# Issuing the last store of a ReLU row-sum kernel from ScalarE instead of SyncE

## The chip, the cores and the metric

The kernel runs on one core of a Trainium2 chip. A core has several engines with instruction streams of their own: VectorE (DVE in the profile), ScalarE (ACT), GpSimd (POOL), TensorE (PE, not used here) and SyncE (SP), which computes nothing and issues DMA transfers. Sixteen DMA engines move the data between HBM and the core's on-chip memory. The streams are ordered against each other by semaphores alone: an instruction can wait until a semaphore has reached a count, and can add to one when it is done; a DMA adds 16 in all when its data has landed.

The metric is the device time of one execution in microseconds, the median over several runs.

## The reference

```python
def setup_inputs():
    batch, seq, dim = 32, 512, 1024
    return {
        "x": np.random.randn(batch, seq, dim).astype(np.float32),
    }

def reference(x: np.ndarray) -> np.ndarray:
    relu_x = np.maximum(x, 0)
    return np.sum(relu_x, axis=-1).astype(np.float32)
```

Every one of the 32 x 512 = 16384 rows of 1024 floats is clamped at zero and summed. 64 MiB are read and 64 KiB are written.

## The kernel before

The rows lie over 128 partitions, 128 rows a partition: sixteen of them from the first eighth of the input, the other 112 from the rest. They are loaded in blocks of 16 rows a partition (8 MiB a load) into three buffers in turn (line 185, `load`); block 3 and those after it wait until VectorE has finished with the buffer. For most blocks ScalarE clamps in place (line 144) and VectorE sums with a reduction (line 152). Towards the end the loads become smaller, 8 and 4 rows (lines 208 to 218), and single rows are clamped and summed in one instruction, by ScalarE (line 159) or VectorE (line 167) alternately.

The last four rows of a partition are cut by hand so that little work is left once the last bytes have landed. Their first two rows and a piece of the third come in one load (line 228); two further pieces are loaded and summed in part by both engines (lines 237 to 243, `act_part` and `dve_part`, lines 121 and 126); the last piece, 403 elements, goes into the buffer `last` (line 244), beside the partial sums. GpSimd clamps one piece ahead (line 234). When all of that is there (`all_there`, line 253), VectorE finishes the sum of row NT - 2 with one instruction (line 254) and ScalarE that of row NT - 1 (line 263). Both add 1 to the semaphore `sems.end`, which then stands at 16 + 5 + 2.

All DMAs are issued by SyncE, in the order of its stream: thirteen loads and then three stores of the sums, from the tile `res` to the output (`store`, lines 110 to 118). The first store holds the first 16 sums of a partition, the second the next 110 and the third the last two (line 264). The third waits for `sems.end` at 16 + 5 + 2. All three add to `sems.stored`.

Behind the last store SyncE goes on to the end block, which is written by hand and holds two instructions: the clear of all the semaphores but `stored` (line 50), which must not happen before the last wait on `sems.end` is over, and a wait until all stores have landed, which also sets `stored` back to zero (line 51):

```python
    nc.sync.sem_clear(cleared)
    nc.sync.wait_ge(sems.stored, 16 * n_stores).then_inc(sems.stored, -16 * n_stores)
```

There are no barriers between the engines in the program; the first load is moved ahead of the program's opening (line 52).

Of the kernel before, what the change touches and what calls it, by code (L numbers as in the profile page):

```python
# [30 lines left out]
def kernel(tc: tile.TileContext, x: bass.AP, out: bass.AP):  # L31
    nc = tc.nc
    sems = Semaphores(tc)

    tc.close()
    tc.compile()
    nc.cur_bb = nc.bb_map[tc.start_bb_name]
    body = nc.cur_bb.bb.instructions
    ends = list(body)
    body.clear()  # L40
    n_stores = relu_sum(nc, sems, x, out)
    body.extend(ends)


    nc.cur_bb = nc.bb_map[tc.start_bb_name + "_end"]
    nc.cur_bb.bb.instructions.clear()
    nums = sorted(s.num for s in (*sems.loads, sems.act, sems.dve))
    cleared = range(nums[0], nums[-1] + 1)
    assert len(cleared) == len(nums)
    nc.sync.sem_clear(cleared)  # L50
    nc.sync.wait_ge(sems.stored, 16 * n_stores).then_inc(sems.stored, -16 * n_stores)
    open_without_barrier(tc, EARLY)


class Semaphores:
    def __init__(self, tc: tile.TileContext):
        n = len(TWO) + len(TAIL) + 4
        self.loads = [tc.alloc_semaphore(f"load{i}") for i in range(n)]
        self.act = tc.alloc_semaphore("act")
        self.dve = tc.alloc_semaphore("dve")  # L60
        self.end = self.loads[-1]
        self.stored = tc.alloc_semaphore("stored")


def relu_sum(nc, sems: Semaphores, x: bass.AP, out: bass.AP):
    x_flat = x.flatten_outer_dims()
    N, D = x_flat.shape
    NT = N // P
# [20 lines left out]
    def rows(m, n):  # L89
        if m < ROWS:  # L90
            return xf[:, m : m + n, :]
        return xv[:, m - ROWS : m - ROWS + n, :]

    def sums(m, n):
        if m < ROWS:
            return of[:, m : m + n], res[:, m : m + n]
        return ov[:, m - ROWS : m - ROWS + n], res[:, m : m + n]
# [12 lines left out]
    def store(m, n, act, sem, count):  # L110
        nonlocal n_store
        dst, src = sums(m, n)
        if act:
            nc.sync.wait_ge(sems.act, act)
        nc.sync.dma_start(out=dst, in_=src).wait_op(sem, count, "sem-ge").then_inc(
            sems.stored, 16
        )
        n_store += 1

    def act_part(ap, accum_out, after):  # L120
        nc.scalar.activation(out=ap, in_=ap, func=RELU, accum_out=accum_out).wait_op(  # L121
            *after, "sem-ge"
        ).then_inc(sems.end, 1)
# [84 lines left out]
    for n in TAIL:  # L208
# [12 lines left out]
    src = rows(m, 4).rearrange("p c d -> p (c d)")  # L221
# [13 lines left out]
        out=clamped, in0=clamped, scalar1=0.0, scalar2=None, op0=MAX  # L235
    ).wait_op(loaded, 16, "sem-ge").then_inc(sems.end, 1)
    for lo, hi, n, first, second in (
# [17 lines left out]
        out=clamped,  # L255
# [5 lines left out]
        accum_out=res[:, NT - 2 : NT - 1],  # L261
    ).wait_op(*all_there, "sem-ge").then_inc(sems.end, 1)
    act_part(last[:, 2 + LAST_DVE :], res[:, NT - 1 : NT], all_there)
    store(NT - 2, 2, 0, sems.end, 16 + 5 + 2)
    return n_store


def open_without_barrier(tc: tile.TileContext, n_loads: int):
# [46 lines left out]
```

## Time and profile before

| What | Value |
|---|---|
| Time, median of 3 runs | 160.91 us (160.89 to 160.95) |
| Span of the profiled execution, first to last instruction | 159.7 us |
| Median less that span | 1.2 us |
| VectorE busy | 118.8 us (74%) |
| ScalarE busy | 103.6 us (65%) |
| GpSimd busy | 1.0 us (1%) |
| DMA | 67.18 MB, one queue, 98.0% of 16 engines' span |
| Last store, 1.0 KB: issue to landing | 1.4 us |

The profiled execution's own time is known as its span, from its first to its last instruction; what lies around the span, start-up and close-down, is in the time of the runs and not in the span. Rows that begin with SPq are instructions of SyncE's sequencer: DMA issues, waits and semaphore operations. The length of a DMA issue is the time that the sequencer needs to hand it over and not that of the transfer, for which the profile gives the time from the issue to the landing.

### The profile page before, as it was taken

How to read it: one execution, taken by the hardware profiler on the slowest of the kernel's cores; microseconds unless marked ns; L12 is line 12 of the kernel's file. 1: busy time of each engine (PE TensorE's matmuls, PEld its weight loads, DVE VectorE, ACT ScalarE, POOL GpSimd, SP SyncE). 2: the span in 40 equal slices, each digit the busy share in tenths (PEclk: the TensorE clock that was granted, in tenths of full speed). 3: DMA queues.
4: the chain of work that ended last, by engine and by line, in shares of the span. 5: the costliest groups of instructions: out<-in, count | busy, mean ns of one | idle time of the engine just before them, and what ended most of it. 6: DMA issues, size and time to landing. Idle time of an engine off the chain costs nothing.

```text
span 159.7 us, 125 instructions
## 1 busy us (share of the span) xinstructions
DVE 118.8 (74%) x44; ACT 103.6 (65%) x53; POOL 1.0 (1%) x5
## 2 busy tenths in 40 slices
DVE  0000000006999799999999999999999799999986
ACT  0000049993699808996099951999329993496995
POOL 0000000000000000000000000000000000000001
DMA  7996996996997997979969969969969969898993
GB/s 263 525 525 263 525 509 279 525 509 279 525 476 312 525 443 345 525 328 460 525 279 509 525 263 525 525 263 525 509 279 525 492 295 525 353 435 386 407 409 128
DMA packets 2304, 67.18 MB, mean 421 GB/s; under 512 B 640, under 2 KB 768, under 8 KB 1024
## 3 DMA queue, kind: packets, MB, share of 16 engines
q1 hardware_dynamic: 2304, 67.18, 98.0%
HBM read 67.11 MB, written 0.07 MB: 421 GB/s over the span
## 4 chain that ended last, share of the span: by engine, by line
DVE 45%; DMA 45%; ACT 9%; SPq 1%; issue 0%
DMA io<-in_x_dram 45%; DVE res L152 43%; ACT io L144 9%; DVE io L167 1%; SPq L103 1%; DVE io L126 1%; DVE io L254 0%
## 5 line engine op out<-in xcount | busy, mean ns | idle before, releaser
L152 DVE TENSOR_REDUCE res<-io 128x8 f32<-128x8192 f32 (+2 forms) x10 | 101.1, 10175 | 38.9 <-ACT io L144 38.9
L144 ACT ACTIVATE io<-io 128x8192 f32<-128x8192 f32 (+2 forms) x10 | 81.8, 8218 | 25.9 <-DMA io<-in_x_dram 25.9
L159 ACT ACTIVATE io<-io 128x1024 f32<-128x1024 f32 x18 | 18.8, 1043 | 6.6 <-DMA io<-in_x_dram 6.6
L167 DVE TENSOR_SCALAR_CACHE_REDUCE io<-io 128x1024 f32<-128x1024 f32 x14 | 16.2, 1214 | 0.5 <-DMA io<-in_x_dram 0.4
L142 ACT ACT_TABLE_LOAD x1 | 1.3, 1283 | 22.0 <-DMA io<-in_x_dram 22.0
L159 ACT ACTIVATION_READ_ACCUMULATOR io<-io 128x1 f32 x18 | 3.4, 187 | 0.0
L234 POOL TENSOR_SCALAR io<-io 128x254 f32<-128x254 f32 x1 | 0.8, 840 | 155.1 <-DMA io<-in_x_dram 155.1
L167 DVE DVE_READ_ACCUMULATOR io<-io 128x1 f32 x14 | 1.1, 82 | 0.0
L126 DVE TENSOR_SCALAR_CACHE_REDUCE io<-io 128x552 f32<-128x552 f32 (+1 forms) x2 | 1.1, 596 | 0.0
L121 ACT ACTIVATE io<-io 128x321 f32<-128x321 f32 (+1 forms) x2 | 0.9, 426 | 0.1
L254 DVE SCALAR_TENSOR_TENSOR io<-last,io 128x254 f32<-128x254 f32 x1 | 0.4, 425 | 0.0
L121 ACT ACTIVATION_READ_ACCUMULATOR io<-io 128x1 f32 x2 | 0.4, 187 | 0.0
L121 ACT ACTIVATE last<-last 128x153 f32<-128x153 f32 x1 | 0.3, 332 | 0.0
L121 ACT ACTIVATION_READ_ACCUMULATOR last<-last 128x1 f32 x1 | 0.2, 187 | 0.0
L126 DVE DVE_READ_ACCUMULATOR io<-io 128x1 f32 x2 | 0.2, 84 | 0.0
L299 POOL MEMSET const-bfloat16-1.0<- 128x1 bf16 x1 | 0.1, 101 | 0.0
L299 POOL MEMSET const-uint8-127<- 128x1 uint8 x1 | 0.1, 101 | 0.0
L299 POOL MEMSET const-float32-0.0<- 128x1 f32 x1 | 0.1, 99 | 0.2 <-issue 0.2
L299 POOL MEMSET const-float32-1.0<- 128x1 f32 x1 | 0.1, 98 | 0.0
L254 DVE DVE_READ_ACCUMULATOR io<-last,io 128x1 f32 x1 | 0.1, 83 | 0.0
## 6 DMA issues: line engine op xcount, KB each, us to landing
io<-in_x_dram SPq DMA_DIRECT2D x1, 4096.0 KB, 23.8
io<-in_x_dram SPq DMA_DIRECT2D x1, 2048.0 KB, 28.3
io<-in_x_dram SPq DMA_DIRECT2D x1, 1151.0 KB, 30.6
io<-in_x_dram SPq DMA_DIRECT2D x1, 436.5 KB, 31.2
io<-in_x_dram SPq DMA_DIRECT2D x1, 259.0 KB, 31.4
last<-in_x_dram SPq DMA_DIRECT2D x1, 201.5 KB, 31.4
io<-in_x_dram SPq DMA_DIRECT2D x7, 29.1
out_dram<-res SPq DMA_DIRECT2D x1, 55.0 KB, 1.6
```

The costliest lines, as they stand in the source:

```text
L103: dma = nc.sync.dma_start(out=dst, in_=src)
L121: nc.scalar.activation(out=ap, in_=ap, func=RELU, accum_out=accum_out).wait_op(*after, "sem-ge").then_inc(sems.end, 1)
L126: i = nc.vector.tensor_scalar(out=ap, in0=ap, scalar1=0.0, scalar2=None, op0=MAX, op1=ADD, accum_out=accum_out,)
L142: nc.scalar.preload_act_table(RELU).wait_op(loaded, 16, "sem-ge")
L144: i = nc.scalar.activation(out=ap, in_=ap, func=RELU)
L152: nc.vector.tensor_reduce(out=res[:, m : m + n], in_=ap, axis=mybir.AxisListType.X, op=ADD).wait_op(sems.act, n_act, "sem-ge").then_inc(se ...
L159: i = nc.scalar.activation(out=ap, in_=ap, func=RELU, accum_out=accum_out)
L167: i = nc.vector.tensor_scalar(out=ap, in0=ap, scalar1=0.0, scalar2=None, op0=MAX, op1=ADD, accum_out=accum_out,)
L234: nc.gpsimd.tensor_scalar(out=clamped, in0=clamped, scalar1=0.0, scalar2=None, op0=MAX).wait_op(loaded, 16, "sem-ge").then_inc(sems.end, 1)
L254: nc.vector.scalar_tensor_tensor(out=clamped, in0=last[:, : 2 + LAST_DVE], scalar=0.0, in1=clamped, op0=MAX, op1=ADD, accum_out=res[:, NT ...
L299: nc = _bacc.Bacc("TRN2", target_bir_lowering=False, num_devices=1)
```

## The change

The third store is no longer issued by SyncE but by ScalarE, from ScalarE's own DMA queue, with the same wait on `sems.end` and the same count on `sems.stored`. SyncE no longer knows by its own wait that `sems.end` is done with; so a new semaphore, `issued`, is added. ScalarE adds 1 to it behind the issue, and SyncE waits for that 1 and takes it back, before it goes on to the clear and to the final wait. The new semaphore is not among those that line 50 clears. SyncE's stream has two stores instead of three, and the count of stores that the final wait asks for is still three.

```diff
@@ -60,6 +60,7 @@
         self.dve = tc.alloc_semaphore("dve")
         self.end = self.loads[-1]
         self.stored = tc.alloc_semaphore("stored")
+        self.issued = tc.alloc_semaphore("issued")
 
 
 def relu_sum(nc, sems: Semaphores, x: bass.AP, out: bass.AP):
@@ -261,8 +262,13 @@
         accum_out=res[:, NT - 2 : NT - 1],
     ).wait_op(*all_there, "sem-ge").then_inc(sems.end, 1)
     act_part(last[:, 2 + LAST_DVE :], res[:, NT - 1 : NT], all_there)
-    store(NT - 2, 2, 0, sems.end, 16 + 5 + 2)
-    return n_store
+    dst, src = sums(NT - 2, 2)
+    nc.scalar.dma_start(out=dst, in_=src).wait_op(
+        sems.end, 16 + 5 + 2, "sem-ge"
+    ).then_inc(sems.stored, 16)
+    nc.scalar.sem_inc(sems.issued, 1)
+    nc.sync.wait_ge(sems.issued, 1).then_inc(sems.issued, -1)
+    return n_store + 1
 
 
 def open_without_barrier(tc: tile.TileContext, n_loads: int):
```

## The prediction

> **What bounds the kernel now.** The body is not touched by the change, so I read the profile from its end. The last pieces of the chain of work that ended last, in order of time (start, length, what):
>
> ```profile
> 124.87 30.59 DMA io<-in_x_dram
> 155.46 0.02 issue
> 155.48 1.23 DVE io L167 x2
> 156.71 1.07 DVE io L126 x4
> 157.78 0.02 issue
> 157.80 0.43 DVE io L254 x2
> ```
>
> The loads end the wait at 155.46 us, then VectorE works to 157.80 + 0.43 = 158.23 us. The span is 159.7 us, so nearly 1.5 us follow in which no engine computes. The timeline of that stretch (start, length, engine and line):
>
> ```profile
> 157.80 0.33 ACT L121 ACTIVATE last<-last 128x153 f32<-128x153 f32 x1
> 157.80 0.42 DVE L254 SCALAR_TENSOR_TENSOR io<-last,io 128x254 f32<-128x254 f32 x1
> 158.04 0.19 ACT L121 ACTIVATION_READ_ACCUMULATOR last<-last 128x1 f32 x1
> 158.15 0.08 DVE L254 DVE_READ_ACCUMULATOR io<-last,io 128x1 f32 x1
> 158.26 0.33 SPq L115 DMA_DIRECT2D out_dram<-res  x1
> ```
>
> ScalarE and VectorE write their last sums within 0.01 us of each other (158.04 + 0.19, 158.15 + 0.08), and SyncE starts to issue the last store 0.03 us later, for 0.33 us. What follows on SyncE is in the rows of its lines (durations min/median/max in ns, first and last start) and in its waits:
>
> ```profile
> L115 SPq DMA_DIRECT2D out_dram<-res x3: 332/344/404, 126.9 to 158.3; - x3
> ...
> DMA to landing us min/median/max: 1.4/1.6/31.0
> ```
>
> ```profile
> L50 SPq EVENT_SEMAPHORE_RANGE_CLEAR  x1: 58/58/58, 158.6 to 158.6; - x1
> ...
> L51 SPq EVENT_SEMAPHORE  x1: 17/17/17, 159.7 to 159.7; - x1
> ```
>
> ```profile
> SPq L115 <- DVE io L254: 1.2, 1, 1.2
> SPq L51 <- SPq L51: 1.0, 1, 1.0
> ```
>
> The clear of the semaphores comes right behind the issue, at 158.6, and is over in 58 ns. Then SyncE waits 1.0 us for the landing, and line 51 at 159.7 is the last instruction of the program. The row above also says that SyncE stood ready for 1.2 us before it could issue the last store. Last, the DMA engines in stretches around that store and around the first load (stretch, its length, engines' busy time, then clock, DMA share and GB/s):
>
> ```profile
> 157.95:159.05 1.10, 0.28 (x2) 0.28 (x2) 0.00 (x0) 1.00 0.00 0
> 159.05:159.30 0.25, 0.00 (x0) 0.00 (x0) 0.00 (x0) 1.00 0.31 4
> 159.30:159.70 0.40, 0.00 (x0) 0.00 (x0) 0.00 (x0) 1.00 0.00 0
> ```
>
> ```profile
> 0.00:0.95 0.95, 0.00 (x0) 0.00 (x0) 0.19 (x4) 1.00 0.00 0
> 1.00:1.10 0.10, 0.00 (x0) 0.00 (x0) 0.00 (x0) 1.00 11.97 3932
> ```
>
> The DMA engines are empty from 157.95 to 159.05; the store's packets run between 159.05 and 159.30 (the packet records: from 159.09); then 0.4 us pass to the landing. So the end of the kernel is: last sum, 0.03; issue to first packet, 0.83 (159.09 - 158.26); packets, 0.20; to the landing, 0.37; line 51, 0.03. The first load, issued at 0.00, has its first packet at 1.015 by the same records.
>
> **The change part by part.** The sum stands against the profiled execution's span, 159.7 us. The median of the timed runs, 160.91, is 1.21 above it: start-up and close-down around the program, which the change does not touch.
>
> The store leaves SyncE's queue: one issue of 332 ns goes, all of it on the path, with its wait for the last sums. Nothing stood behind it but the clear and the final wait.
>
> It comes back on ScalarE with the same wait, behind ScalarE's last read of its accumulator (ends 158.23). ScalarE has no later work, so nothing is queued behind the wait except its own end. Waking: SyncE needed 0.03 us; ScalarE and VectorE both started at 157.80 on the landing that let them go at 157.75 in the semaphore records. I take 0.
>
> The issue: an issue that SyncE had ready while it waited took 327 to 344 ns (lines 103 and 115); one that followed straight on another took 404 to 466. ScalarE's has its wait ahead of it like the first kind, so 332 ns is the nearest and the difference 0; from the other kind it is at most 466 - 332 = +0.13.
>
> Issue to first packet: 0.83 for the last store and the same for the one before (156.73 to 157.57 in the packet records); 1.015 for the very first DMA of SyncE's queue, +0.19. The last store is equal in size and direction; the first load is equal in that it is the first of its queue, as the store will be on ScalarE's. Of the 0.19, 0.05 is the longer issue (383 against 332 ns), counted above. The two rows each fit in one respect, so I take a value between, +0.10. A gain can't be excluded: if the first packet left as soon as the issue ended, at 0.33, it would be -0.49, for which no row speaks. Packets and landing move the same 1.0 KB to the same place: 0.
>
> By the Trainium skill's "DMA: Bandwidth & Descriptors", section "Latency and other measured facts", a DMA issued from SP or ACT has its first byte after about 600 ns, on either queue; the estimate from that page would be 0.83 - 0.60 = 0.23 less, 160.68. The trace does not agree for SyncE's queue (0.83 and 1.015), and no row shows ScalarE's.
>
> The handshake: ScalarE adds 1 to a semaphore after its issue (end near 158.26 + 0.33 + 0.10 = 158.69 at the latest forecast), SyncE wakes (0.03), takes it back (17 ns, as line 51), goes to the clear (158.64 - 158.59 = 0.05 behind the issue today) and clears (0.06). All of that, some 0.2 us with the increment, ends by 158.9 and the landing is at 159.7 or later, so it costs nothing: it hides under the store's own flight, with about 0.8 us to spare. If that cover went, each microsecond of hand-over beyond it would be one of time. SyncE's earlier loads and stores keep their places; the store at 156.73 is still issued ahead of this one. POOL's queue has nothing at the end (its last work stops at 156.4).
>
> Sum: +0.10, span 159.8, time 160.91 + 0.10 = 161.01.
>
> **The rivals.** The measurement of this kernel can tell about 0.2% from no change, here 0.32 us: faster is below 160.59, slower above 161.23.
>
> First rival, slower: ScalarE's sequencer is the dearer place to issue from. Place: between 158.23 and the first packet. All row bounds together, +0.13 and +0.14, give 161.18, just inside; it decides once ScalarE's path costs over 0.32 more than SyncE's. An issue twice as long as the longest of SyncE's (0.93 for 0.33) gives +0.60, 161.5. For it: no row shows a DMA from ScalarE, and its 53 instructions are all compute. Against it: same transfer, and DMA engines empty.
>
> Second rival, faster: the new queue starts sooner. SyncE's queue still had the store of 156.73 in flight until 158.29 (1.6 us to landing in the rows above), which overlaps the issue of the last one; if an empty queue cuts 0.4 of the 0.83, the time is 160.5. Against it: the first load found an empty queue and took longer, 1.015, and the packets of the earlier store were done by 157.91. The same page, under "Issuing engines are not separate DMA queues", says that issuing from several engines saves the sequencer's issue time alone; here SyncE was free 1.2 us ahead, so by that there is nothing to gain and the time is 160.91.
>
> Third, slower: the hand-over takes over 1 us instead of 0.2, and SyncE reaches line 51 after the landing. At 1.4 us it would end 0.3 to 0.4 late, 161.3. Nothing in the rows of semaphore instructions (17 and 58 ns) speaks for it. With it I count an unseen cost outside the span.
>
> **How the numbers follow.** Forecast, 161.01 within 160.8 to 161.23: 0.63. First rival 0.23, third 0.04: slower 0.27. Second 0.10: faster 0.10. The range runs from 160.75, which takes in a small gain, to 161.5, the first rival's priced case; it leaves out the second rival and the far end of the first and third, under 2 in 10.
>
> **What would show it.** The list of queues must have a second one with 128 packets, and the last issue stand on ScalarE near 158.26. Right: an issue of 0.33 to 0.47 there, landing 1.4 to 1.7 after it, the clear near 158.9, and line 51's counterpart still waiting for the landing. Wrong: a late or long issue on ScalarE or a first packet more than 1.15 after it (first rival), a landing in 1.0 (second), or a SyncE whose last wait is for ScalarE's semaphore and not for the store (third). Any change ahead of 157.8 would be another cause than these.

## The result, and the profile after

| | before | after |
|---|---|---|
| Median | 160.91 us (160.84 to 161.18, 9 runs) | 161.30 us (161.23 to 161.50, 9 runs) |
| Ratio | | 1.0025, 95% interval 1.0015 to 1.0034 |
| Span of the profiled execution | 159.7 us | 159.7 us |

The change costs 0.39 us, and the spans show little of it. The nine executions after the change have spans of 159.6 to 159.8 us, and their time less their span is 1.62 to 1.70 us, in the mean 1.67. Of the kernel before, 97 executions were timed with their spans, beside the experiments below: their time less their span is 1.29 to 1.39 us, in the mean 1.35. (These spans are known to 0.1 us, so up to 0.05 us of the scatter either way is rounding.) So some 0.33 of the 0.39 us, by the means before rounding, lie outside the span, and no execution of the one kernel comes near those of the other. The 1.2 us given for the kernel before set the median of the timed runs against the span of one execution, which was a long one: its span is 159.70 us, where the 97 have a mean of 159.63.

The end of the kernel after the change, in order of time (start, length, engine and line):

```profile
157.70 0.33 ACT L122 ACTIVATE last<-last 128x153 f32<-128x153 f32 x1
157.70 0.42 DVE L255 SCALAR_TENSOR_TENSOR io<-last,io 128x254 f32<-128x254 f32 x1
157.93 0.19 ACT L122 ACTIVATION_READ_ACCUMULATOR last<-last 128x1 f32 x1
158.05 0.08 DVE L255 DVE_READ_ACCUMULATOR io<-last,io 128x1 f32 x1
158.16 0.37 ACTq L266 DMA_DIRECT2D out_dram<-res  x1
```

The issue stands on ScalarE's sequencer, 0.03 us behind VectorE's last sum as it did on SyncE. Everything here is 0.10 us earlier than in the profile before, mostly because in this execution the last load landed 0.08 us earlier; the part of the kernel that the change does not touch moves by such amounts from one profile to the next (the last issue starts at 158.02 to 158.33 in thirteen of the fourteen profiles of this study). That is why the span is no longer although the store is slower. The row of the store's line, with its time to the landing in us:

```profile
L266 ACTq DMA_DIRECT2D out_dram<-res x1: 373/373/373, 158.2 to 158.2; - x1
...
DMA to landing us min/median/max: 1.5/1.5/1.5
```

Its issue takes 373 ns against 332, its landing 1.455 us against 1.399 in the records: +0.056. SyncE's waits, and the rows of the two semaphore instructions of the handshake and of the clear:

```profile
SPq L270 <- SPq L270: 1.6, 1, 1.6
SPq L51 <- SPq L51: 0.9, 1, 0.9
```

```profile
L269 ACTq EVENT_SEMAPHORE  x1: 17/17/17, 158.6 to 158.6; - x1
```

```profile
L270 SPq EVENT_SEMAPHORE  x1: 17/17/17, 158.6 to 158.6; - x1
```

```profile
L50 SPq EVENT_SEMAPHORE_RANGE_CLEAR  x1: 52/52/52, 158.7 to 158.7; - x1
```

SyncE now waits for ScalarE's semaphore (line 270) where it waited for the last sums, clears at 158.7 us, and still waits 0.9 us for the landing. So the handshake is hidden with that much to spare. The DMA queues:

```profile
q1 hardware_dynamic: 2160, 67.17, 97.9%
q10 hardware_dynamic: 144, 0.00, 0.0%
```

The second queue is ScalarE's, with the last store alone on it: 144 packets, where the prediction had asked for 128. In the packet records 128 of them carry 8 bytes each and 16 carry 4; the same store on SyncE's queue had the same 144.

What is left to explain is the 0.33 us that lie outside the span.

### The profile page after: what moved, and what is told of

The parts are those of the page before. It is cut to its first block, busy times and chain, and to the rows that moved or that the text cites. A ratio compares the mean times of both kernels' runs of the same rounds, so it can differ in the third digit from the quotient of the medians.

```text
span 159.7 us, 127 instructions
## 1 busy us (share of the span) xinstructions
DVE 118.7 (74%) x44; ACT 103.6 (65%) x53; POOL 1.0 (1%) x5
## 4 chain that ended last, share of the span: by engine, by line
DVE 45%; DMA 45%; ACT 9%; SPq 1%; issue 0%
DMA io<-in_x_dram 45%; DVE res L153 43%; ACT io L145 9%; DVE io L168 1%; SPq L104 1%; DVE io L127 1%; DVE io L255 0%
```

## The experiments

All stand against the kernel before, run beside them on the same chip (median 160.94 for the first four, 160.97 for the others); ratios have 95% intervals. "Time less span" is the mean over all executions of a kernel, with a standard error of about 0.01 us; for the kernel before it is 1.35. The mean span of the kernel before is 159.61 us beside the first four, 159.63 beside the next four and 159.65 beside the last four; a mean span has a standard error of 0.02 to 0.06 us. Three suspects at first: the use of a second queue as such (theory 1), the last store's place on ScalarE (theory 2), the handshake (theory 3); theories 4 to 6 came from results.

**A second queue, away from the end.**

```diff
+    scratch = nc.alloc_sbuf_tensor("scratch", [P, 2], F32)
+    nc.scalar.dma_start(out=scratch[:, 0:2], in_=xf[:, 0, 0:2]).then_inc(sems.warm, 16)
...
+    nc.sync.wait_ge(sems.warm, 16).then_inc(sems.warm, -16)
     store(0, ROWS, freed[0][0], sems.dve, freed[0][1])
```

> The kernel before, with one added load of 1.0 KB into a scratch tile that nobody reads, issued by ScalarE as its first instruction, where it stands idle for 22 us; SyncE takes its semaphore back at 126.8 us, where it waits anyway. The last store stays on SyncE and there is no handshake. Theory 1 (a program that uses ScalarE's queue at all pays some 0.35 to 0.45 us outside the span, whatever is issued there and when): time 161.25 to 161.35, span 159.6 to 159.8 as before, time less span up from 1.2 to about 1.6 us. Theory 2 (the cost comes from the last store itself being issued late from ScalarE): 160.9, time less span 1.2.

161.29 us, ratio 1.0022 (1.0013 to 1.0031), time less span 1.58, which is 0.23 above the kernel before; the mean span is 159.74, 0.12 above. The added DMA stands at the very start, and the last store is SyncE's:

```profile
0.12 0.38 ACTq L184 DMA_DIRECT2D scratch<-in_x_dram  x1
```

Most of the cost outside the span is there without the store's move, so theory 2 is not the whole of it. At this point theory 1 looked confirmed, although it had put all of the 0.35 us outside the span.

**The handshake alone.**

```diff
+    nc.scalar.sem_inc(sems.issued, 1)
     store(NT - 2, 2, 0, sems.end, 16 + 5 + 2)
+    nc.sync.wait_ge(sems.issued, 1).then_inc(sems.issued, -1)
```

> The kernel before, with the handshake alone: ScalarE adds 1 to a new semaphore behind its last instruction, SyncE issues the last store itself, waits for the 1 and takes it back, then clears. Theory 1 (use of ScalarE's queue): 160.9, time less span 1.2, because no second queue is used; SyncE's two more instructions end some 0.06 us later, within the store's flight. Theory 3 (the new semaphore and SyncE's extra wait cost it): 161.2 or more.

161.11 us, ratio 1.0012 (1.0004 to 1.0021), time less span 1.49. No theory expected this half-way result: no second queue, an end of the kernel that shows nothing late (issue to landing 1.400 us), and still 0.17 us, 0.14 of them outside the span.

**ScalarE's store without the handshake.**

```diff
-    nc.scalar.sem_inc(sems.issued, 1)
-    nc.sync.wait_ge(sems.issued, 1).then_inc(sems.issued, -1)
+    nc.sync.wait_ge(sems.end, 16 + 5 + 2)
...
     nc.sync.wait_ge(sems.stored, 16 * n_stores).then_inc(sems.stored, -16 * n_stores)
+    nc.sync.wait_ge(sems.end, 16 + 5 + 2).then_inc(sems.end, -(16 + 5 + 2))
```

> The last store issued by ScalarE as in the change, without the handshake: SyncE waits itself for the last sums, clears all the semaphores but the one that ScalarE's issue waits for, waits for the landing, and takes that one back with one more instruction at the end (some 0.05 us in the span). Theory 1 (use of ScalarE's queue): 161.3 to 161.4, time less span about 1.6. Theory 3 (handshake): back to 160.95. Theory 2 (late issue from ScalarE) 161.3 as well.

161.32 us, ratio 1.0024 (1.0015 to 1.0034), time less span 1.57; the instruction added at the end makes the span 0.1 us longer than the landing needs. The total is that of the change, but it is made up in another way: time less span is 0.11 below the change's (1.53 to 1.61 us in its ten executions, 1.62 to 1.70 after the change), and the longer span hides that. So leaving out the handshake did gain 0.11 us outside the span; the other 0.22 stay, and theory 3 does not explain them.

**The change with ScalarE's queue used before.** The scratch load of the first experiment, added to the change.

> The change with the 1.0 KB scratch load on ScalarE's queue at the start added, so that the last store is no longer the first DMA of that queue. In the span: if the 0.05 us that ScalarE's store takes longer from issue to landing (1.46 against 1.40) is a first use, it goes and issue to landing is 1.40; if it is ScalarE's own issue (373 against 332 ns), 1.46 stays. Outside: Theory 1 with a price for each queue: 161.3, time less span 1.6 as after the change; Theory 1 with a price for each DMA on it: another 0.4, 161.7. Theory 2: 161.3.

161.28 us, ratio 1.0022 (1.0013 to 1.0030), time less span 1.47. Two DMAs on the queue cost no more than one in the total, but here too the total hides two movements. Time less span is 0.20 below the change's, although ScalarE issues one DMA more, and the mean span is 159.85, 0.24 above the kernel before. In the span the row of the store:

```profile
L274 ACTq DMA_DIRECT2D out_dram<-res x1: 349/349/349, 158.2 to 158.2; - x1
...
DMA to landing us min/median/max: 1.4/1.4/1.4
```

The issue takes 349 ns and the landing 1.418 us, against 373 and 1.455 for the same store as its queue's first DMA (372 and 1.445 in the run without the handshake), and 332 or 333 and 1.395 to 1.405 for SyncE's last store in the eleven profiles that have it. So about 0.03 of the 0.05 us belong to the first use of the queue and the rest to an issue from ScalarE; the second use is seen in this one profile.

**The same scratch load on SyncE's queue.**

```diff
+        if j == NBUF:
+            nc.sync.dma_start(out=scratch[:, 0:2], in_=xf[:, 0, 0:2]).then_inc(sems.warm, 16)
```

> The kernel before with the same added scratch load of 1.0 KB as in the run with a scratch load on ScalarE's queue, but issued by SyncE on its own queue, behind its third load, where it waits for VectorE for some 50 us anyway. Theory 1 (a second queue in use costs): 160.9, no second queue. Rival (any added DMA, semaphore and wait costs the 0.35): 161.3.

161.06 us, ratio 1.0006 (0.9997 to 1.0015), time less span 1.35. The total is not to be told from no change, and outside the span nothing moves: a DMA, a semaphore and a wait more are not enough by themselves. The mean span, 159.73, is 0.10 above the kernel before, much as with the same load on ScalarE's queue.

**One more semaphore, unused.**

```diff
+        self.issued = tc.alloc_semaphore("issued")
```

> The kernel before with one more semaphore allocated and used by no instruction: the same instructions in the same order. Every theory of a mechanism expects 160.94; if it reads 161.1 as the run with the handshake alone did, then 0.17 us is what a rebuild can move, and no more can be said of the handshake.

160.96 us, ratio 1.0001 (0.9992 to 1.0010), time less span 1.35. Its instructions are those of the kernel before, and nothing moves; as far as one such kernel shows, the 0.17 us of the handshake are more than what a rebuild can move.

**The handshake early.**

```diff
+    nc.scalar.sem_inc(sems.issued, 1)
     freed = []
...
+    nc.sync.wait_ge(sems.issued, 1).then_inc(sems.issued, -1)
     store(0, ROWS, freed[0][0], sems.dve, freed[0][1])
```

> The handshake alone, far from the end: ScalarE adds 1 as its first instruction, SyncE takes it back ahead of the first store at 126.8 us. If the 0.17 us of the handshake alone come from its place behind the last store: 160.94. If they come from the instructions being in the two streams at all: 161.1. Theory 1 (second queue): no second queue, 160.94.

161.18 us, ratio 1.0011 (1.0002 to 1.0020), time less span 1.54, and the span is that of the kernel before (159.63). The handshake alone costs no less at the beginning than at the end (1.49): its place is not the cause. Its being in the streams seemed to be.

**The scratch load on ScalarE's queue, one partition.** `scratch[0:1, 0:2]` from `xf[0:1, 0, 0:2]`.

> The scratch load on ScalarE's queue cut to 8 bytes for one partition, so that one DMA engine works for it and not sixteen. Theory 1 with a price for the queue: 161.3, as with 1.0 KB. Theory 1 with a price for each of the sixteen engines' rings that was used: close to 160.95.

161.15 us, ratio 1.0013 (1.0004 to 1.0022), time less span 1.50. Between the two expectations: the queue is used, by two packets, and outside the span that costs what one semaphore instruction on ScalarE cost (1.49 and 1.54). The mean span, 159.64, is that of the kernel before, so the 0.10 to 0.12 us in the span came with the 144 packets of the full load.

**The early handshake from VectorE.** `nc.vector.sem_inc` in the place of `nc.scalar.sem_inc`.

> The early handshake with VectorE in the place of ScalarE: VectorE adds 1 as its first instruction, SyncE takes it back ahead of the first store. Theory 4 (one more sequencer instruction in ScalarE's stream costs 0.15 to 0.2 us outside the span): 160.95, as the stream is VectorE's. Theory 5 (any engine's added instruction, or SyncE's added wait, costs it): 161.15.

161.02 us, ratio 1.0005 (0.9996 to 1.0014), time less span 1.35. Outside the span nothing moves: SyncE's wait is not the cause, and an instruction more on VectorE is not either.

**One more activation on ScalarE.**

```diff
     act_part(last[:, 2 + LAST_DVE :], res[:, NT - 1 : NT], all_there)
+    nc.scalar.activation(out=scratch[:, :], in_=last[:, 2:3], func=RELU)
```

> The kernel before with one more activation of one element a partition into a scratch tile, behind ScalarE's last one, with no wait and no semaphore; it ends near 158.6 us, within the last store's flight. Theory 4 with the length of ScalarE's stream as the cause: 161.1. Theory 4 with a sequencer instruction (semaphore or DMA) as the cause: 160.95. Theory 5: 161.1 if any added instruction counts, 160.95 if SyncE's wait does.

161.15 us, ratio 1.0012 (1.0003 to 1.0021), time less span 1.51. In its timeline the added instruction (line 265) is over while SyncE is still issuing the last store:

```profile
158.20 0.18 ACT L265 ACTIVATE scratch<-last 128x1 f32<-128x1 f32 x1
158.22 0.08 DVE L255 DVE_READ_ACCUMULATOR io<-last,io 128x1 f32 x1
158.33 0.33 SPq L116 DMA_DIRECT2D out_dram<-res  x1
```

No semaphore, no DMA, no second queue, nothing on the path, the mean span as before, and yet 0.16 us more outside the span.

**Four semaphore instructions on ScalarE.** The early handshake, with `sem_inc` four times and SyncE waiting for 4.

> The early handshake with ScalarE adding 1 four times, in four instructions, and SyncE waiting once for 4. Theory 4 with a price for each instruction: 160.95 + 4 x 0.17, about 161.6. A step paid once: 161.15. Noise of the build: 160.95.

160.99 us, ratio 1.0000 (0.9991 to 1.0009), time less span 1.35. Four instructions cost nothing where one cost 0.2 us: theory 4 falls, with a price for each instruction as with a step.

**Four scratch loads on ScalarE's queue.**

> Four scratch loads of 1.0 KB on ScalarE's queue at the start in place of one. Theory 1 with a price for the queue: 161.3, as with one. With a price for each DMA or each instruction: 161.3 plus 3 times 0.17 to 0.35, 161.8 to 162.3.

161.39 us, ratio 1.0021 (1.0009 to 1.0032), time less span 1.36. The total is what theory 1 expected, but it lies elsewhere, in the span: the eight executions have spans of 159.7 to 160.2 us, in the mean 160.00, which is 0.35 above the kernel before. The queues of this run, and the span of the profiled execution, the longest of the eight:

```profile
q1 hardware_dynamic: 2304, 67.18, 97.7%
q10 hardware_dynamic: 576, 0.00, 0.2%
```

```profile
core 0: 160.2 us, clock 1.000
```

Its chain of work that ended last, in order of time, has a first stretch of loads of 41.19 us (first row) where the profile before has 40.86 (second row):

```profile
0.43 41.19 DMA io<-in_x_dram
```

```profile
0.43 40.86 DMA io<-in_x_dram
```

In this execution the last load lands 0.5 us later than in the profile before (158.25 against 157.75 in the records). In the mean over executions it is 0.35 us for four scratch loads, about 0.09 for each; one such load made the mean span longer by 0.12 us from ScalarE's queue and by 0.10 from SyncE's. So this part goes with the added load and not with the queue that it stands on. Time less span is as low as in the kernel before, in all eight executions (1.32 to 1.41), so ScalarE's queue can be used, with four DMAs, without the cost outside the span. Theory 1 falls as well.

**What all of them have in common.** The trace has 53 instructions of ScalarE before and 55 after the change. Sorted by that number (the change's span stands against the mean of all 97 executions of the kernel before, the others' against those run beside them):

| ScalarE's instructions | kernel | time less span, us | mean span less before, us |
|---|---|---|---|
| 53 | the kernel before | 1.35 | |
| 53 | unused semaphore | 1.35 | -0.01 |
| 53 | SyncE's scratch load | 1.35 | 0.10 |
| 53 | VectorE's handshake | 1.35 | 0.04 |
| 54 | handshake | 1.49 | 0.09 |
| 54 | 1-partition load | 1.50 | 0.01 |
| 54 | extra activation | 1.51 | 0.00 |
| 54 | early handshake | 1.54 | 0.00 |
| 54 | store without handshake | 1.57 | 0.17 |
| 54 | scratch load | 1.58 | 0.12 |
| 55 | the change | 1.67 | 0.04 |
| 56 | the change with the scratch load | 1.47 | 0.24 |
| 57 | four semaphore instructions | 1.35 | 0.01 |
| 57 | four scratch loads | 1.36 | 0.35 |

Theory 6 is that the time around the span goes with the length of ScalarE's stream, with a period of four: 53 and 57 are lowest, 55 highest. It was formed after these runs and none was left to test it, above all not 55 without a second queue, or the change lengthened to 57. The single executions bear the sorting out: with 53 and 57 instructions all of them lie between 1.29 and 1.41 us, with the other numbers none below 1.43. But the length is not all. The six kernels with 54 differ by 0.09, more than standard errors of 0.01 allow, and the two highest are the two that use ScalarE's queue for a full-size DMA; so a part of the queue's own, of some 0.06 us, is not excluded.

The trace shows nothing that would be the mechanism. In all fourteen profiles a close series of semaphore records begins 2.66 to 2.79 us ahead of the first instruction. The last semaphore records stand 1.43 to 1.46 us behind the last instruction in thirteen of them, those of the lowest and of the highest time less span included, and at 1.58 in the change with the scratch load. The packets that the trace marks as instruction DMA all lie ahead of the first instruction, and there are thirteen of them with the unused semaphore (1.35) as after the change (1.67); the profile before has eleven.

## Why the prediction was right or wrong

The measured 161.30 lies in the range of 160.75 to 161.5, and 0.29 above the forecast of 161.01. The case that was given 0.63, 160.8 to 161.23, is not met by the median and not excluded by the interval, which is 161.15 to 161.46 us. That the time lies in the range is luck: the range went up to 161.5 for the first rival, whose mechanism did not happen, and most of the cost came from a place at which the sum had nothing. The signs that were named for being right came true in the main (the issue, the landing, the last wait; the clear came 0.2 us sooner), and none of them could see that place. Its steps:

- "start-up and close-down around the program, which the change does not touch": this is the step that failed. The body of the program is untouched, but time less span went from 1.35 to 1.67, +0.33 before rounding, most of the 0.39. The prediction's 1.21 for it was too low as well, because it came from the median of some executions and the span of another. The prediction had "an unseen cost outside the span" with the third rival, at 0.04 and with no price.
- The issue, priced at 0 to +0.13: +0.041 (373 against 332). It stayed below the 404 to 466 ns of an issue that follows another, as the wait ahead of it had suggested.
- Issue to first packet, +0.10 taken between 0 and +0.19: 159.034 - 158.163 = 0.871 in the packet records, +0.046 with the longer issue in it. A first use does cost, as the first load's row suggested, but less. The rest of the way takes 0.01 us more than before, so in the span the sum was +0.10 and measured +0.056.
- The Trainium skill's figure of about 600 ns to the first byte ("DMA: Bandwidth & Descriptors", section "Latency and other measured facts") is not what either queue shows from the start of the issue: 0.825 us from SyncE and 0.871 from ScalarE. From the end of the issue it is 0.49 and 0.50, and the page does not say from where it counts.
- The handshake: the clear ends at 158.74 us, forecast by 158.9, and the wait for the landing still has 0.9 us. Hidden as said; but as instructions in the streams it went with 0.14 and 0.19 us more outside the span in the two kernels that have it alone, with ScalarE adding 1 once, which no step had.
- First rival, ScalarE the dearer place by over 0.32: the total is of that size, but the mechanism did not happen, its place has +0.056.
- Second rival, a sooner start: did not happen. The Trainium skill's section that it was weighed with ("DMA: Bandwidth & Descriptors", "Issuing engines are not separate DMA queues") lets nothing but the sequencer's issue time be saved by issuing from several engines, and the trace agrees: nothing was gained.
- Third rival, the hand-over reaches the end: did not happen.

The total of +0.056 and +0.33 is +0.38, against 0.39 measured. Shown is where the cost lies, in every execution. What sets it stays open: that it is the length of ScalarE's stream is a reading of the table and not shown.

## What to carry to other kernels

Here the tail was the last store's own flight of 1.40 us, and moving that store to another engine's queue did not shorten it; as the first DMA of its queue it landed some hundredths of a microsecond later. When a change is worth only tenths of a microsecond, split the time of every execution into its span and the rest: the rest scattered by 0.1 us here, where the totals of the kernel before scattered by 0.8, and totals that looked alike (the change, the store without the handshake, the scratch load) were made up of different parts. Run a control that adds an instruction with no work to do: here such a control moved the time by up to 0.2 us, as much as the effects in question. One confirming run is not enough either: the first experiment's total fitted the second-queue theory, and the run with four DMAs on that queue took it away.

## What the runs showed of the hardware

- The time around the span is not a constant of the chip: its means are 1.35 to 1.67 us over fourteen kernels that differ by a few instructions, and the executions of the kernel before (1.29 to 1.39) and after (1.62 to 1.70) do not overlap.
- One activation of one element, over before the last store's issue was, made the kernel 0.18 us slower (1.0003 to 1.0021), 0.16 of it outside the span, while four semaphore instructions made it no slower (0.9991 to 1.0009).
- A store of 1.0 KB from ScalarE landed 1.455 and 1.445 us after the start of its issue as the first DMA of its queue and 1.418 as the second; from SyncE 1.395 to 1.405 in eleven profiles.
- A load of 1.0 KB in 144 packets beside the large loads made the mean span 0.12 us longer from ScalarE's queue and 0.10 from SyncE's, four of them 0.35; a load of two packets made no difference that shows (0.01).
